# A hybrid decoder layer on one core: the value convolution's shifts from SBUF to SBUF in two rounds, and the inverse's natural rows read during the substitution

## The chip, the cores and the metric

The kernel runs on one core of a Trainium2 chip. The metric is the device time of one execution in microseconds. Each time shown is a median of runs on the chip; the profile is of one separate execution, with its own time beside it.

## The reference, cut to what matters

One layer, 256 tokens of width 2048, 256 memory tokens, float32. One projection of the normalised tokens gives q, k, v and two gates for a gated DeltaNet (24 value heads, 12 query and key heads of 128), the queries of a 4-head cross-attention into the memory, and a gate path z of width 4096. The branches are joined, multiplied by SiLU of z and sent through an output projection into the residual.

```
qkv = jax.nn.silu(causal_depthwise_conv(p[..., :c_qkv], conv_w))   # 4 taps along the tokens
m   = jnp.where(strict, beta * kk * decay, 0.0) + eye              # lower triangular, one per head and chunk
sol = lax.linalg.triangular_solve(m, rhs, left_side=True, lower=True, unit_diagonal=True)
y   = jnp.concatenate([mix, xa], axis=-1) * jax.nn.silu(z)
x   = x + jnp.einsum("bse,ed->bsd", y, w_out[i])
```

Two steps matter here. The depthwise convolution adds to each token's value three earlier tokens' values, each times a weight of its channel. And the triangular system of each head has to be inverted.

## The kernel before, in words

**Stream.** All weights flow through one pipeline, in the order of PLAN (line 55 on): blocks of 128 x 1024 numbers are loaded by SyncE's DMA queue into one of five `st` buffers (wraw, 278), cast on ScalarE into the upper part of one of four `wt` buffers (line 335), and VectorE subtracts to get the lower part (line 339). TensorE multiplies with both parts; twelve matmuls of 512 columns use up a block of the kinds V, K, x, v, z and o (proj_b), and a q or k tile takes two blocks (proj_a). LOOK keeps a few blocks ahead.

**Order.** The program is one stream of instructions, written by a small scheduler in Python. The big products set its clock `now`. Side work (convolutions, the inverse, the recurrence `delta`, the cross-attention) runs as generators that give up control with `yield`: a number is a delay in modelled microseconds, `pe_soon` (234) waits for what has been issued plus SLACK and then joins the queue for TensorE with a delay GATHER, `calm` (247) waits until VectorE's modelled backlog is under CALM. Each engine then executes its instructions in exactly the order in which they were written, and so does SyncE with its copies. Almost all operations are recorded through two helpers, so they have the lines 86 (TensorE, SyncE) and 103 (the others) in the profile; tiles are told apart by name.

**Values.** A v tile g (six of them) covers 512 value channels. Its matmuls end in two PSUM banks, one for each half r of 128 tokens, tokens on partitions (`v_done`, 1161). Since the tokens lie on partitions, a shift by tokens is a shift by partitions. For each half the value block `vs` is copied from PSUM, stored into a DRAM scratch `dv` with three rows of zeros ahead, and read back three times at offsets of one, two and three rows (`vsh`). Four weight rows, broadcast to all partitions, are loaded as `vw`. VectorE then does four products and three sums of 128 x 512, ScalarE the SiLU. `delta(g)` needs the two halves. `taps` (1147) prepares the weights in DRAM (`dtap`) and the rows of zeros in `dv`.

**Inverse.** `inverse(g)` runs twice, for 12 heads and two chunks each. `gram` writes the scaled matrices to DRAM (`dN`). The diagonal blocks of 32 x 32 are inverted by substitution on VectorE (`inN`, `inXT`, 31 steps), go through DRAM (`dY`, `dX`) into `Y` and `XN`, and then the natural rows of the whole matrices are read back as six tiles `n` of 128 x 512 (`n2`). After LAND, `merge` (1007) builds the 128 x 128 inverses on TensorE: 96 small matmuls `pm<-Y,n`, 72 pairs `pm<-Am,XN` and `pm<-XN,Am`, 48 + 48 larger ones. The second merge waits until `delta(2)` has used the first's `Y`.

Of the kernel before, what the change touches and what calls it, by code (L numbers as in the profile page):

```python
# [8 lines left out]
F32 = mybir.dt.float32  # L9
F32R = mybir.dt.float32r  # L10
AF = mybir.ActivationFunctionType
ALU = mybir.AluOpType
# [10 lines left out]
C = 128  # L23
# [9 lines left out]

LOOK = 2
WARM = 8
GATHER = 2.0
GATHER_Y = 4.0
XPACE = 3.0
HOP = 0.25
PINNED = 45.0  # L40
SLACK = 0.7
POLL = 0.3
CALM = 1.6
LAND = 6.0
VLAND = 5.0
INV_CALM = (1.2, 1.2)
GATE_CALM = 1.6
# [8 lines left out]
for _s in ("K0 K1 ab0 x0 x1 k0 k1 k2 k3 k4 k5 z6 z7 z0 z1 k6 k7 k8 v0 q0 q1 k9 k10 k11 v1 q2 q3 z2 v2 q4 q5 z3 v3 q6 q7 v4 q8 q9 v5 q10 q11 z4 z5 o0 o1 o2 o3").split():  # L56
    _kind = _s.rstrip("0123456789:")
    _t, _, _n = _s[len(_kind) :].partition(":")
# [14 lines left out]
def hybrid_kernel(ctx: ExitStack, tc: tile.TileContext, x, xT, memT, W, prm_d, cst_d, out):  # L73
# [51 lines left out]
    ve, se = Engine(nc.vector, ve_cost), Engine(nc.scalar, se_cost)  # L125
    po = Engine(nc.gpsimd, lambda e, op, a, k: 0.6)
# [8 lines left out]
    sd = Transfers()  # L135
# [7 lines left out]
    dp = ctx.enter_context(tc.tile_pool(name="dp", bufs=1, space=DRAM))  # L143

    def S2(name, shape, dt=F32):
        return s2p.tile([128] + list(shape), dt, name=name, tag="s2")
# [26 lines left out]
    def give(pt, t):  # L173

        idle[held.pop(id(pt))[0]].append(t)

    def bank(tag, name):
        yield from until(lambda: spare(tag))
        return PS(tag, name)
# [22 lines left out]
    def tr(o_, i_):  # L202
        now[0] += 0.093
        te.transpose(o_, i_, ident)
# [25 lines left out]
    def until(cond):  # L230
        while not cond():
            yield POLL

    def pe_soon(gather=0.0):

        yield max(fin[0] - now[0], 0.0) + SLACK
        yield "pe", gather
# [9 lines left out]
    def calm(queued=CALM):  # L247

        while ve.end > now[0] + queued:
            yield ve.end - now[0] - queued  # L250
# [677 lines left out]
    dN = [dp.tile([24, 129 * C], F32, name=f"dN{g}", tag=f"dN{g}") for g in range(2)]  # L928
# [3 lines left out]
    def mat(t):  # L932
        return t[:, 0 : C * C].rearrange("s (r c) -> s r c", c=C)

    def diag(t):

        return (t.rearrange("s (k e) -> (s k) e", k=4)[:, 0 : 32 * C]
                .rearrange("p (r c) -> p r c", c=C)[:, :, 0:32])

    def inverse(g):  # L940
        yield from until(lambda: all(p in grams for p in range(6 * g, 6 * g + 6)) and (g == 0 or "sub" in ready))
        yield 0.5
        nn = [S2("inN", [16, 32])[0:96] for _ in range(2)]
        xt = [S2("inXT", [16, 32])[0:96] for _ in range(2)]
        for f in range(2):
            sd.dma_start(nn[f], diag(dN[g])[:, 16 * f : 16 * f + 16])
        for f in range(2):
            po.memset(xt[f], 0.0)
        yield
        for f in range(2):  # L950
            po.memset(xt[f].rearrange("s c r -> s (c r)")[:, 16 * f : 512 : 33], 1.0)
        yield
        for i in range(1, 32):
            yield from calm(INV_CALM[g])
            work = []
            for f in range(2):
                w, j0 = min(16, i - 16 * f), 16 * f
                if w > 0:
                    tm = S2("inT", [16 * 32])[0:96]
                    work.append((f, w, j0, tm[:, 0 : w * (i - j0)].rearrange("s (c j) -> s c j", c=w)))  # L960
            for f, w, j0, tv in work:
                ve.tensor_tensor(out=tv, in0=xt[f][:, 0:w, j0:i],
                                 in1=nn[i // 16][:, i % 16, j0:i].unsqueeze(1).to_broadcast([96, w, i - j0]), op=ALU.mult)
            for f, w, j0, tv in work:
                ve.tensor_reduce(out=xt[f][:, 0:w, i], in_=tv, axis=AX.X, op=ALU.add)
            if len(work) == 1:
                ve.run(0.25)
        yield
        ready.add("sub")
        xn = nn  # L970
        for f in range(2):
            for e in range(2):
                ve.tensor_copy(xn[e][:, :, 16 * f : 16 * f + 16], xt[f][:, :, 16 * e : 16 * e + 16].rearrange("s c r -> s r c"))
        yield
        for f in range(2):
            sd.dma_start(dY[g][:, 16 * f : 16 * f + 16], xt[f])
        for f in range(2):
            sd.dma_start(dX[g][:, 16 * f : 16 * f + 16], xn[f])
        yield
        yield from until(lambda: g == 0 or "y5" in ready)  # L980
        nat = dX[g].rearrange("(s k) r c -> k r s c", k=4)
        tsp = dY[g].rearrange("(s k) r c -> k r s c", k=4)
        for k in range(4):
            b = slice(32 * k, 32 * k + 32)
            sd.dma_start(yall[b, :, b], tsp[k])
        for e in range(2):
            for k, r0, c0 in ((0, 64 * e, 0), (1, 64 * e + 32, 32), (2, 96 - 64 * e, 0)):
                sd.dma_start(xall[r0 : r0 + 32, e, :, c0 : c0 + 32], nat[k][:, 12 * e : 12 * e + 12])
        n2 = [S2("n2", [4, C]) for _ in range(6)]
        for i in range(6):  # L990
            sd.dma_start(n2[i], mat(dN[g])[4 * i : 4 * i + 4].rearrange("s r c -> r s c"))
        yield LAND
        yield from merge(g, n2)

# [147 lines left out]
    vss = [None] * 6  # L1142

    dtap = dp.tile([96, 128], F32, name="dtap", tag="dtap")
    dv = [dp.tile([259, 512], F32, name=f"dv{i}", tag=f"dv{i}") for i in range(2)]

    def taps():
        pt = yield from bank("m", "ptap")
        tr(pt[0:96, 0:128], prm[:, P_CW + 96 : P_CW + 192])
        yield 0.2  # L1150
        tp = S2("tp", [512])
        ve.memset(tp[:, 128:512], 0.0)
        se.copy(tp[0:96, 0:128], pt[0:96, 0:128])
        give(pt, se.end)
        yield
        sd.dma_start(dtap, tp[0:96, 0:128])
        for i in range(2):
            sd.dma_start(dv[i][0:3, 0:384], tp[0:3, 128:512])
            sd.dma_start(dv[i][0:3, 384:512], tp[0:3, 128:256])

    def v_done(g):

        raw, w = [None] * 2, []

        def done(r, pt):
            def go():
                yield 0.2
                v = raw[r] = S2("vs", [512])
                se.copy(v, pt)
                give(pt, se.end)  # L1170
                yield
                sd.dma_start(dv[g % 2][3 + 128 * r : 131 + 128 * r], v)
                if r == 0:
                    for j in range(4):
                        w.append(S2("vw", [4, 128]))
                        sd.dma_start(w[j], dtap.rearrange("(t k) c -> k t c", k=4)[3 - j][4 * g : 4 * g + 4]
                                     .unsqueeze(0).to_broadcast([128, 4, 128]))
                yield VLAND
                sh = [S2("vsh", [512]) for _ in range(3)]
                for j in (1, 2, 3):  # L1180
                    sd.dma_start(sh[j - 1], dv[g % 2][3 + 128 * r - j : 131 + 128 * r - j])
                wf = [t.rearrange("c t e -> c (t e)") for t in w]
                ve.tensor_tensor(out=v, in0=v, in1=wf[0], op=ALU.mult)
                yield VLAND
                for j in (1, 2, 3):
                    yield from calm()
                    ve.tensor_tensor(out=sh[j - 1], in0=sh[j - 1], in1=wf[j], op=ALU.mult)
                    ve.tensor_tensor(out=v, in0=v, in1=sh[j - 1], op=ALU.add)
                yield
                se.activation(v, v, AF.Silu)  # L1190
                vv = v.rearrange("c (w e) -> c w e", w=4)
                yield from until(lambda: all(p in grams for p in (2 * g, 2 * g + 1)))
                for h in range(4):
                    se.activation(vv[:, h, :], vv[:, h, :], AF.Copy, scale=sV[:, r, 4 * g + h : 4 * g + h + 1])
                yield
                raw[r] = vv
                ready.add(f"v{g}{r}")
                if r == 1:
                    vss[g] = raw
                    yield from delta(g)  # L1200
            spawn(go())
        return done

# [5 lines left out]
    def delta(g):  # L1209
# [6 lines left out]
        heads = [(w, w // 2, w % 2) for w in range(4)]  # L1216
        yield from pe_soon(GATHER)

# [16 lines left out]
        for i, p in enumerate(pp):  # L1235
            ve.tensor_tensor(out=kcl[:, i], in0=pkv[i][:, 0:4:2, :], in1=kch[:, i], op=ALU.subtract)
            give(pks[i], ve.end)
        yield from pe_soon(GATHER)
        A = yield from bank("A", "pU")
# [15 lines left out]
        ve.tensor_tensor(out=ul, in0=u0f, in1=uh, op=ALU.subtract)  # L1255
        yield from pe_soon(GATHER)
        yield from until(lambda: spare("A") and spare("B"))
# [17 lines left out]
        give(B, se.end)  # L1275
        yield from pe_soon(GATHER)
        yield from until(lambda: spare("A", 2))
# [13 lines left out]
        for i, p in enumerate(pp):  # L1291
            se.activation(q2[:, i, :], KQ[p][:, 1, :], AF.Square)
        yield from pe_soon(GATHER)
        yield from until(lambda: spare("B") and spare("m"))
# [179 lines left out]
```

## Time and profile before

| | |
|---|---|
| median of 3 runs | 873.8 us (873.25 to 876.49) |
| the profiled execution, its own time | 871.74 us |
| its span | 869.9 us |
| mean granted TensorE clock | 0.992 |
| busy: TensorE, VectorE, ScalarE, GpSimd | 854.2, 618.8, 535.7, 31.1 us |
| DMA | 187.9 MB, 216 GB/s over the span |
| copies of values: `dv<-vs`, `vsh<-dv`, `vw<-dtap` | 12, 36 and 24, of 256 KB each |
| natural rows `n<-dN` | 12 of 256 KB, issued from 317.6 to 543.1 us |

The first merge lies at 327 to 352 us of the span, the second at 549 to 566. The v tiles are worked on VectorE from about 349 to 654 us, between q tiles, z tiles and the recurrence; after 725 us there is only the output projection. A row of a group has the line, engine, operation, tiles written and read, shapes and count, then busy time and the mean of one in ns, then the idle time just before them and what ended it. A row of the windows has the length, the busy time of the engines with the number of instructions, the granted clock (1.00 is full), the busy share of the 16 DMA engines and GB/s. "issue" is time in which an engine waited for nothing that the profile shows.

### The profile page before, as it was taken

What the parts mean: (1) busy time and instruction counts of PE and PEld (TensorE: products, weight loads), DVE (VectorE), ACT (ScalarE), POOL (GpSimd) and SP (SyncE); (2) the same over time, 40 slices, a digit from 0 to 9 for tenths busy, and PEclk for the clock granted to TensorE, in tenths of its full rate; (3) what the DMA queues carried; (4) which work ended last, traced back from release to release, by engine and by line L of the source; (5) the groups of instructions that cost most, each with busy time, mean ns of one, the idle gap of its engine ahead of it and who ended that gap; (6) DMA issues with size and microseconds to landing.
All of it is one profiled execution on the core that took longest, in us unless ns stands there. A gap on an engine that the chain in (4) does not pass through costs nothing.

```text
span 869.9 us, 13113 instructions
## 1 busy us (share of the span) xinstructions
PE 854.2 (98%) x4789; PEld 716.0 (82%) x4789; DVE 618.8 (71%) x1081; ACT 535.7 (62%) x925; POOL 31.1 (4%) x33
## 2 busy tenths in 40 slices
PE   9999999999999998999999999799999999999998
PEld 6888888888888887888888888687888888888886
DVE  7778896657779954897988997359695665454542
ACT  7655755797644754896765775578776554333331
POOL 1000000000000000001000000000000000000000
PEclk9999999999999998999999999899999999999999
DMA  9865556448676686869869569767954538666650
GB/s 354 300 206 184 168 182 173 151 152 253 198 209 225 206 238 235 292 197 331 238 207 299 176 218 271 243 221 240 296 185 151 181 132 272 218 199 210 202 204 24
DMA packets 148239, 187.91 MB, mean 216 GB/s; under 512 B 24652, under 2 KB 115664, under 8 KB 148176
## 3 DMA queue, kind: packets, MB, share of 16 engines
q1 hardware_dynamic: 147744, 186.81, 66.5%
q8 instruction: 37, 0.61, 0.3%
q10 hardware_dynamic: 432, 0.28, 0.1%
q14 instruction: 26, 0.21, 0.1%
HBM read 177.01 MB, written 10.05 MB: 215 GB/s over the span
## 4 chain that ended last, share of the span: by engine, by line
PE 89%; ACT 5%; DMA 2%; issue 2%; DVE 2%; SPq 0%; POOL 0%; ACTq 0%; DVEq 0%
PE pb L86 68%; PE pa L86 12%; PE pO L86 2%; PE pU L86 1%; ACT wt L335 1%; PE pm L86 1%; ACT L103 1%; PE pkq L86 1%; ACT dec L103 1%; DVE wt L339 1%; DMA dv<-vs 1%; DMA vw<-dtap 1%; PE pyT L86 1%; PE pqs L86 1%; PE pkk L86 1%
## 5 line engine op out<-in xcount | busy, mean ns | idle before, releaser
L339 DVE TENSOR_TENSOR wt<-st,wt 128x1024 fp32r<-128x1024 f32 (+1 forms) x274 | 332.1, 1217 | 161.1 <-ACT wt L335 150.4
L335 ACT CAST wt<-st 128x1024 fp32r<-128x1024 f32 (+1 forms) x274 | 285.9, 1048 | 223.7 <-PE pb L86 184.1
L86 PE MATMUL pb<-wt,hkt 128*128 128x512 f32 x1536 | 361.6, 393 | 0.0
L86 PEld LDWEIGHTS pb<-wt,hkt 128*128 128x128 f32 x1536 | 286.7, 189 | 59.2
L86 PE MATMUL pb<-wt,yhi 128*128 128x512 f32 x512 | 158.1, 390 | 0.0
L86 PE MATMUL pa<-hkt,wt 128*128 128x512 f32 (+1 forms) x768 | 143.5, 343 | 0.4 <-DVE wt L339 0.3
L86 PEld LDWEIGHTS pa<-hkt,wt 128*128 128x128 f32 x768 | 118.9, 190 | 18.7 <-DVE wt L339 1.1
L86 PEld LDWEIGHTS pb<-wt,yhi 128*128 128x128 f32 x512 | 95.7, 188 | 19.6
L86 PE MATMUL pb<-wt,ylo 128*128 128x512 f32 x256 | 99.6, 389 | 0.0
L86 PE MATMUL pb<-wt,mkt 128*128 128x512 f32 x384 | 92.0, 400 | 0.9 <-ACT wt L335 0.7
L86 PEld LDWEIGHTS pb<-wt,mkt 128*128 128x128 f32 x384 | 73.6, 193 | 18.2 <-ACT wt L335 1.5
L86 PEld LDWEIGHTS pb<-wt,ylo 128*128 128x128 f32 x256 | 48.0, 188 | 10.1
L103 ACT ACT_TABLE_LOAD x29 | 37.2, 1283 | 5.7 <-DVE acc L103 5.3
L103 DVE SCALAR_TENSOR_TENSOR acc<-raw,prm,acc 128x255 f32<-128x255 f32 (+2 forms) x72 | 34.4, 478 | 1.4 <-ACT acc L103 1.0
L103 DVE TENSOR_TENSOR inT<-inXT,inN 96x1 f32<-96x1 f32 (+22 forms) x92 | 29.1, 342 | 3.0 <-DMA inN<-dN 2.3
L103 DVE TENSOR_REDUCE inXT<-inT 96x1 f32<-96x1 f32 (+22 forms) x92 | 28.6, 337 | 0.8
L103 DVE TENSOR_TENSOR vsh<-vsh,vw 128x512 f32<-128x512 f32 x36 | 24.1, 686 | 3.1 <-DMA vsh<-dv 3.1
L103 DVE TENSOR_TENSOR vs<-vs,vsh 128x512 f32<-128x512 f32 x36 | 24.7, 685 | 0.1
L103 POOL TENSOR_TENSOR e<-e,mhalf 128x8 f32<-128x8 f32 x6 | 10.5, 1748 | 288.9 <-DVE e L103 202.3
L103 ACT ACTIVATE dec<-erow,ngc 128x128 f32<-128x128 f32 x48 | 16.0, 394 | 4.0 <-DMA erow<-dgc 2.3
L103 ACT ACTIVATE dec<-erow,gcc 128x128 f32<-128x128 f32 x48 | 15.9, 396 | 3.5 <-DMA erow<-dgc 3.5
L103 DVE TENSOR_TENSOR vs<-vs,vw 128x512 f32<-128x512 f32 x12 | 8.2, 690 | 13.8 <-DMA dv<-vs 6.2
(202 smaller groups left out, 678.8 us busy)
## 6 DMA issues: line engine op xcount, KB each, us to landing
st<-W_d SPq DMA_DIRECT2D x272, 512.0 KB, 4.4
vsh<-dv SPq DMA_DIRECT2D x36, 256.0 KB, 6.2
erow<-dgc SPq DMA_DIRECT2D x24, 256.0 KB, 5.8
vw<-dtap SPq DMA_DIRECT2D x24, 256.0 KB, 6.0
dN<-dec SPq DMA_DIRECT2D x12, 256.0 KB, 2.9
n<-dN SPq DMA_DIRECT2D x12, 256.0 KB, 5.3
dv<-vs SPq DMA_DIRECT2D x12, 256.0 KB, 4.8
xraw<-xT_d SPq DMA_DIRECT2D x8, 256.0 KB, 5.7
```

The source lines that it names most:

```text
L86: return lambda *a, **k: pin(getattr(self.eng, op)(*a, **k))
L103: return pin(getattr(self.eng, op)(*a, **k))
L335: pin(se.eng.copy(hi[:, w] if parts > 1 else hi, st[:, w] if parts > 1 else src))
L339: pin(ve.eng.tensor_tensor(out=lo[:, w] if parts > 1 else lo, in0=st[:, w] if parts > 1 else src, in1=hi[:, w] if parts > 1 else hi, op=AL ...
```

## The change

Three things are changed, and three numbers.

The values' shifts no longer go through DRAM. With x1 the block shifted by one token, the four-tap sum is (w3 v + w2 x1), plus (w1 v + w0 x1) shifted by two tokens. So the first round copies `vs` one partition down inside SBUF (rows 0 to 126 to rows 1 to 127; the first row comes from the last row of the other half, or is a fill with zeros), and the second round copies the sum `t` two partitions down (126 rows, and two). The scratch `dv` and its rows of zeros are gone. The `vw` loads are issued before the values' copy.

The six natural row tiles `n` are requested one by one, from step 20 of the substitution, every second step, instead of all after the copies of `Y` and `XN`.

LAND, the time that a merge is held after its copies, goes from 6.0 to 9.0, SLACK from 0.7 to 1.0, GATHER, used in `delta`, from 2.0 to 0.5.

```
-GATHER = 2.0
+GATHER = 0.5
...
-SLACK = 0.7
+SLACK = 1.0
...
-LAND = 6.0
+LAND = 9.0
...
+            if i >= 20 and i % 2 == 0:
+                n2.append(S2("n2", [4, C]))
+                k = 4 * len(n2)
+                sd.dma_start(n2[-1], mat(dN[g])[k - 4 : k].rearrange("s r c -> r s c"))
...
-        n2 = [S2("n2", [4, C]) for _ in range(6)]
-        for i in range(6):
-            sd.dma_start(n2[i], mat(dN[g])[4 * i : 4 * i + 4].rearrange("s r c -> r s c"))
         yield LAND
...
-    dv = [dp.tile([259, 512], F32, name=f"dv{i}", tag=f"dv{i}") for i in range(2)]
...
+        def shift(dst, src, r, n):
+
+            sd.dma_start(dst[n:128], src[r][0 : 128 - n])
+            if r:
+                sd.dma_start(dst[0:n], src[0][128 - n : 128])
+            else:
+                po.memset(dst[0:n], 0.0)
...
                 yield
-                sd.dma_start(dv[g % 2][3 + 128 * r : 131 + 128 * r], v)
...
+                a, y, t = [S2("vc", [512]) for _ in range(3)]
+                shift(a, val, r, 1)
                 yield VLAND
-                sh = [S2("vsh", [512]) for _ in range(3)]
-                for j in (1, 2, 3):
-                    sd.dma_start(sh[j - 1], dv[g % 2][3 + 128 * r - j : 131 + 128 * r - j])
...
+                yield from calm()
...
+                ve.tensor_tensor(out=t, in0=v, in1=w1, op=ALU.mult)
+                ve.tensor_tensor(out=y, in0=a, in1=w0, op=ALU.mult)
+                ve.tensor_tensor(out=t, in0=t, in1=y, op=ALU.add)
+                two[r] = t
+                yield
+                yield from until(lambda: two[0] is not None)
+                b = S2("vc", [512])
+                shift(b, two, r, 2)
+                yield from calm()
+                ve.tensor_tensor(out=y, in0=v, in1=w3, op=ALU.mult)
+                ve.tensor_tensor(out=a, in0=a, in1=w2, op=ALU.mult)
+                ve.tensor_tensor(out=y, in0=y, in1=a, op=ALU.add)
                 yield VLAND
-                for j in (1, 2, 3):
-                    yield from calm()
-                    ve.tensor_tensor(out=sh[j - 1], in0=sh[j - 1], in1=wf[j], op=ALU.mult)
-                    ve.tensor_tensor(out=v, in0=v, in1=sh[j - 1], op=ALU.add)
+                yield from calm()
+                v = y
+                ve.tensor_tensor(out=v, in0=y, in1=b, op=ALU.add)
```

SyncE's queue at the first v tile, before: the stores and loads of the scratch, between weight loads (`st`), decay rows (`erow`) and the weights of the taps (`vw`).

```order
L86 DMA erow<-dgc 128x512
L86 DMA dv_113<-vs 128x512
L86 DMA vw<-dtap 128x4x128 x4
L86 DMA erow<-dgc 128x512
L86 DMA dv_113<-vs 128x512
L86 DMA st<-W_d 128x1024
L86 DMA vsh<-dv_113 128x512 x3
L86 DMA st<-W_d 128x1024
L86 DMA vsh<-dv_113 128x512 x3
```

The same place now; `vc` are the tiles of the new rounds.

```order
L86 DMA vw<-dtap 128x4x128 x4
L86 DMA st<-W_d 128x1024
L86 DMA erow<-dgc 128x512
L86 DMA vc<-vs 127x512 x2
L86 DMA vc<-vs 1x16x32
L86 DMA erow<-dgc 128x512
L86 DMA st<-W_d 128x1024 x3
L86 DMA st<-W_d 128x4x256
L86 DMA vc<-vc 126x512
L86 DMA erow<-dgc 128x512
L86 DMA st<-W_d 128x4x256
L86 DMA vc<-vc 126x512
```

The two copies of 127 rows, one for each half, stand next to each other, and each 126-row copy has weight loads before and behind it.

VectorE at the same place, before: `raw` and `acc` are the convolution of the q tile that follows.

```order
L339 TENSOR_TENSOR wt<-st,wt 128x1024 x6
L103 TENSOR_TENSOR vs<-vs,vw 128x512 x2
L103 TENSOR_TENSOR raw<-raw 128x256
L103 TENSOR_TENSOR vsh<-vsh,vw 128x512
L103 TENSOR_TENSOR vs<-vs,vsh 128x512
L103 TENSOR_TENSOR vsh<-vsh,vw 128x512
L103 SCALAR_TENSOR_TENSOR acc<-raw,prm,acc 128x255
L103 TENSOR_TENSOR vs<-vs,vsh 128x512
L103 SCALAR_TENSOR_TENSOR acc<-raw,prm,acc 128x254
L339 TENSOR_TENSOR wt<-st,wt 128x1024
```

VectorE now:

```order
L339 TENSOR_TENSOR wt<-st,wt 128x1024 x6
L103 TENSOR_TENSOR vc<-vs,vw 128x512
L103 TENSOR_TENSOR vc<-vc,vw 128x512
L103 TENSOR_TENSOR raw<-raw 128x256
L103 TENSOR_TENSOR vc<-vc 128x512
L103 TENSOR_TENSOR vc<-vs,vw 128x512
L103 TENSOR_TENSOR vc<-vc,vw 128x512
L103 SCALAR_TENSOR_TENSOR acc<-raw,prm,acc 128x255
L103 TENSOR_TENSOR vc<-vc 128x512
L103 SCALAR_TENSOR_TENSOR acc<-raw,prm,acc 128x254
L339 TENSOR_TENSOR wt<-st,wt 128x1024
```

The first `vc<-vc,vw` reads the first half's 127-row copy, the second the other half's; no subtraction of a weight block stands between the two.

SyncE's queue ahead of the second merge, before: the six `n` come after `Y` and `XN`, in one run.

```order
L86 DMA vsh<-dv_114 128x512 x3
L86 DMA Y<-dY_107 32x24x32 x4
L86 DMA XN<-dX_109 32x12x32 x6
L86 DMA n_5384<-dN_105 128x4x128
L86 DMA n_5385<-dN_105 128x4x128
L86 DMA n_5386<-dN_105 128x4x128
```

Now they lie between weight loads, ahead of the copies into `dY`:

```order
L86 DMA n_4967<-dN_105 128x4x128
L86 DMA st<-W_d 128x4x256 x2
L86 DMA n_5004<-dN_105 128x4x128
L86 DMA erow<-dgc 128x512
L86 DMA st<-W_d 128x1024
L86 DMA erow<-dgc 128x512
L86 DMA n_5078<-dN_105 128x4x128
L86 DMA st<-W_d 128x1024 x3
```

The last of the six stands between the two 127-row copies of the fourth v tile.

More of the change, by code (lines that the diff above doesn't have):

```diff
@@ L952, in inverse @@
         yield
+        n2 = []
         for i in range(1, 32):
@@ L1150, in taps @@
         yield 0.2
-        tp = S2("tp", [512])
-        ve.memset(tp[:, 128:512], 0.0)
-        se.copy(tp[0:96, 0:128], pt[0:96, 0:128])
+        tp = S2("tp", [128])
+        se.copy(tp[0:96], pt[0:96, 0:128])
         give(pt, se.end)
         yield
[L1156 to L1159, printed above, removed]
+        sd.dma_start(dtap, tp[0:96])
     def v_done(g):
-        raw, w = [None] * 2, []
+        raw, w, val, two = [None] * 2, [], [None] * 2, [None] * 2
+        def shift(dst, src, r, n):
[4 more added lines that the diff above has]
+                po.memset(dst[0:n], 0.0)
         def done(r, pt):
@@ L1167, in go @@
                 yield 0.2
-                v = raw[r] = S2("vs", [512])
+                v = val[r] = S2("vs", [512])
                 se.copy(v, pt)
                 give(pt, se.end)
-                yield
-                sd.dma_start(dv[g % 2][3 + 128 * r : 131 + 128 * r], v)
                 if r == 0:
@@ L1177, in go @@
                                      .unsqueeze(0).to_broadcast([128, 4, 128]))
+                yield
+                a, y, t = [S2("vc", [512]) for _ in range(3)]
+                shift(a, val, r, 1)
                 yield VLAND
-                sh = [S2("vsh", [512]) for _ in range(3)]
-                for j in (1, 2, 3):
-                    sd.dma_start(sh[j - 1], dv[g % 2][3 + 128 * r - j : 131 + 128 * r - j])
-                wf = [t.rearrange("c t e -> c (t e)") for t in w]
-                ve.tensor_tensor(out=v, in0=v, in1=wf[0], op=ALU.mult)
+                yield from calm()
+                w3, w2, w1, w0 = [t_.rearrange("c t e -> c (t e)") for t_ in w]
+                ve.tensor_tensor(out=t, in0=v, in1=w1, op=ALU.mult)
+                ve.tensor_tensor(out=y, in0=a, in1=w0, op=ALU.mult)
+                ve.tensor_tensor(out=t, in0=t, in1=y, op=ALU.add)
+                two[r] = t
+                yield
+                yield from until(lambda: two[0] is not None)
[5 more added lines that the diff above has]
+                ve.tensor_tensor(out=y, in0=y, in1=a, op=ALU.add)
                 yield VLAND
-                for j in (1, 2, 3):
-                    yield from calm()
-                    ve.tensor_tensor(out=sh[j - 1], in0=sh[j - 1], in1=wf[j], op=ALU.mult)
-                    ve.tensor_tensor(out=v, in0=v, in1=sh[j - 1], op=ALU.add)
+                yield from calm()
+                v = y
+                ve.tensor_tensor(out=v, in0=y, in1=b, op=ALU.add)
                 yield
```

## The prediction

> **What bounds the kernel now.** I read the page's busy shares first, then the chain that ended last, the waits, the windows of 20 us, and the DMA part.
>
> ```profile
> span 869.9 us, 13113 instructions
> PE 854.2 (98%) x4789; PEld 716.0 (82%) x4789; DVE 618.8 (71%) x1081; ACT 535.7 (62%) x925; POOL 31.1 (4%) x33
> PE 89%; ACT 5%; DMA 2%; issue 2%; DVE 2%; SPq 0%; POOL 0%; ACTq 0%; DVEq 0%
> 725.39 140.79 PE pb L86 x621
> 551.83 4.61 issue
> ```
>
> TensorE is busy 98% of the span, and the chain runs through it for 89%. The last piece of the chain gives its undisturbed pace: 140.79 us over 621 matmuls is 0.227 us each, so a weight block of 12 matmuls lasts 2.72 us. Whatever leaves TensorE fed costs nothing; whatever starves it adds to the time one for one.
>
> ```profile
> 320.00:340.00 20.00, 16.91 (x299) 14.27 (x298) 7.51 (x19) 8.93 (x18) 1.01 (x1) 0.83 0.73 248
> 520.00:540.00 20.00, 20.00 (x119) 17.55 (x118) 14.86 (x26) 11.39 (x25) 0.00 (x0) 1.00 0.93 286
> 540.00:560.00 20.00, 14.82 (x287) 12.27 (x286) 11.91 (x24) 11.36 (x29) 1.64 (x1) 0.88 0.92 296
> 560.00:580.00 20.00, 19.87 (x172) 15.97 (x171) 7.93 (x8) 16.13 (x31) 0.00 (x0) 0.95 0.36 112
> ```
>
> After the span's first slices the two real holes are the merges, at 330 to 338 and 549 to 557 us (columns: PE, PEld, DVE, ACT, POOL, granted clock, DMA share, GB/s). In each, TensorE stood still for some microseconds and then ran at a lower granted clock: 0.83 of 20 us is 3.4 us lost, and 0.88 with 0.95 is 2.4 + 1.0 = 3.4 us. So a hole of 4 to 5 us costs itself and 3.4 us of slow clock.
>
> ```profile
> ACT wt L335 <- PE pb L86: 184.1, 134, 3.5
> DVE wt L339 <- ACT wt L335: 150.4, 119, 5.4
> SPq L86 <- DVE wt L339: 391.1, 171, 10.9
> L339 DVE TENSOR_TENSOR wt<-st,wt 128x1024 fp32r<-128x1024 f32 (+1 forms) x274 | 332.1, 1217 | 161.1 <-ACT wt L335 150.4
> L335 ACT CAST wt<-st 128x1024 fp32r<-128x1024 f32 (+1 forms) x274 | 285.9, 1048 | 223.7 <-PE pb L86 184.1
> ```
>
> This is the cover that feeds it. The cast of a block waits 134 times for TensorE to free one of the four wt buffers: three blocks lie between a freed buffer and its next use, 3 x 2.72 = 8.2 us, of which cast and subtraction take 1.05 + 1.22. A finished block is thus at most 5.9 us early, and 3.2 us just before the next is made: 4.5 us on average. If VectorE stops, TensorE runs dry some 4.5 us later.
>
> **What the change does to the copies.** The DRAM round goes: 12 stores of values and 36 shifted loads. In their place stand 12 copies of 127 rows, 12 of 126 and twelve of one or two rows. How long does a 127-row copy take?
>
> ```profile
> DMA packets 148239, 187.91 MB, mean 216 GB/s; under 512 B 24652, under 2 KB 115664, under 8 KB 148176
> q1 hardware_dynamic: 147744, 186.81, 66.5%
> q10 hardware_dynamic: 432, 0.28, 0.1%
> ...
> st<-W_d SPq DMA_DIRECT2D x272, 512.0 KB, 4.4
> ...
> dv<-tp SPq DMA_DIRECT2D x2, 4.5 KB
> dv<-tp SPq DMA_DIRECT2D x2, 1.5 KB
> dgc<-gc SPq DMA_DIRECT2D x1, 24.0 KB
> ...
> dgl<-gc SPq DMA_DIRECT2D x1, 0.1 KB
> glb<-dgl SPq DMA_DIRECT2D x1, 12.0 KB
> ```
>
> The packet counts tell how rows are shared out. Queue 10 carried three copies of 128 rows: 432 = 3 x 128 + 3 x 16, so each ends in 16 small packets, one per engine. Now all packets under 512 B: 24,652, less 16,896 rows of 128 B (8 Y copies x 768, 12 XN x 384, 4 inN x 1,536), 128 rows of glb, 128 of prm and 24 elements of dgl, leaves 7,476 closing packets. The list of issues has 471 copies. The 465 of 32, 96 or 128 rows give 7,440; the 36 left are four copies of 3 rows with 3 each and the two of 24 rows with 12 each. So 24 rows run on 12 engines, two each, not on 16. Every copy in the program has equal shares on at most 16 engines. 127 is a prime: its only equal share is all on one engine. Rounded-up shares (8 rows on 15 engines, 7 on the last) would explain the 24 rows as well; no copy here tells these apart. I take equal shares, since nothing else was ever seen.
>
> The Trainium skill ("DMA: Bandwidth & Descriptors", section "Why a DMA increments its semaphore by 16 and not by 1") says that a copy issued from SyncE takes the largest number up to 16 that divides the rows, and that 127 rows go to one engine. The closing packets agree with it for 3 and 24 rows; by rounding up instead, the sum would be that of the first rival.
>
> ```profile
> 554.00:556.00 2.00, 0.00 (x0) 0.81 1.02 403
> DMA to landing us min/median/max: 3.0/5.6/7.5
> ```
>
> The first row is a 2 us window of TensorE (clock, DMA share, GB/s): 403 GB/s at 1.02 of 16 engines is 24.7 GB/s an engine; queue 1 over the run gives 186.81 MB / (0.665 x 16 x 869.9 us) = 20.2. 127 rows of 2 KB are 260,096 B: 10.5 us on one engine, or 12.9. The second row is that of the tile dv: its copies land 3.0 us after issue at best, of which 0.7 is moving, so 2.3 us come on top. The first copy lands 12.8 us after issue. The second (the other half of the tokens) stands right behind it on SyncE and on the same engine: 23.3 us. I take the faster rate, since these are long packets.
>
> ```profile
> 347.28 1.37 SPq L86 DMA_DIRECT2D vsh<-dv  x3
> 354.37 0.68 DVE L103 TENSOR_TENSOR vsh<-vsh,vw 128x512 f32<-128x512 f32 x1
> L103 DVE TENSOR_TENSOR vsh<-vsh,vw 128x512 f32<-128x512 f32 x36 | 24.1, 686 | 3.1 <-DMA vsh<-dv 3.1
> ```
>
> VectorE uses a shifted copy some 7.1 us after its issue (VLAND is still 5.0 and the calm limit 1.6); for copies landing in 6.2 us that was right, and it waited 3.1 us in all. Now it stands from +7 until +12.8 for the first copy, and then, with no subtraction of a weight block between the two products in five groups of six, until +23.3 for the second. Behind it lie the q tile's additions and the subtractions that feed TensorE. On SyncE the 126-row copy waits for VectorE's sum, with weight loads behind it; loads that were issued have a sixteenth of their rows behind the two copies on that engine.
>
> TensorE runs dry at 7 + 4.5 = 11.5 and gets its next block at 23.3 + two more operations of 0.69 + 1.22, about 26: 14.5 us idle. With the longest cover (5.9) and a block squeezed in between (2.72), and the subtraction next in line, it is 24.5 - 15.6 = 8.9. I take the middle, 11.7, and 3.4 us of slow clock: 15.1 us a group, 90.6 us for six. Ends: 6 x 8.9 = 53; with 12.9 us a copy, the second landing at 28.1, 6 x (30.7 - 11.5 + 3.4) = 136.
>
> **The other parts.** VectorE's work on the values stays: seven operations of 0.69 us a half, before and after. The 12 fills on GpSimd are some 0.3 us each on an engine busy 4%: nothing. The bytes fall by 24 x 256 KB, 3% of 187.9 MB, hidden while TensorE is full.
>
> ```profile
> DVE vs L103 <- DMA dv<-vs: 6.2, 3, 2.6
> DVE vs L103 <- DMA vw<-dtap: 5.5, 4, 2.5
> PE pU L86 <- DVE ul L103: 0.9, 1, 0.9
> PE pm L86 <- issue: 6.0, 2, 4.6
> q8 instruction: 37, 0.61, 0.3%
> ```
>
> The waits of VectorE that go (6.2 and, as vw is now asked for before the shift, 5.5) stand where TensorE was full: 520 to 540 has 20.00 of 20. I count nothing, 1 us of gain at most. GATHER and SLACK place delta's matmuls about 1 us sooner; TensorE's longest wait there was 0.9 us, so -1 to +3, taken as 0.
>
> The natural inverse rows (six copies of 256 KB a merge) now go out between weight loads, and LAND holds the merge 3 us more; SyncE waited 391 us for VectorE anyway, so their issue is covered. What do they save? TensorE's 4.61 us in the second merge stood in the middle of one run of 72 small matmuls, behind no semaphore. PE has 2 x 4789 instructions; 37 packets on the instruction queue are one per 259 of them, so this is most likely a late block of instructions, while DMA stood at 1.02. In the first merge, with DMA quieter, that wait was shorter:
>
> ```profile
> 334.25 0.53 PE L86 MATMUL pm<-Am,XN 32*32 32x32 f32 x19 [1.42 <-issue]
> 556.44 0.25 PE L86 MATMUL pm<-Am,XN 32*32 32x32 f32 x1 [4.61 <-issue]
> ```
>
> With 1.5 MB less in flight I take the second down to the first: -3.2. Ends: 0, and -8 if hole and slow clock both go. The Trainium skill ("Runtime: NRT & Kernel Launch", section "Instruction fetch mechanics") calls crossing such a block mostly hidden; the 4.61 us speak against that here, and by the page this term would be 0.
>
> **Sum.** On the profiled execution, 871.7 us with 869.9 of span: 871.7 + 90.6 - 3.2 = 959. It lies 2 us below the median of the runs shown, 873.8; I do not add them. About 0.5%, 4.4 us, is what a measurement can tell from no change.
>
> **The rivals.** *Rounded-up shares, faster.* The 127 rows go as 8 to an engine and land like dv's copies, at 5.6 us; VectorE's wait stays nil. Then the merges (-3.2, perhaps -8) and up to 1 us of removed waits remain: 871.7 - 3.2 - 1 = 867.5, between 862 and 871. For it: 24 rows on 12 engines fits. Against it: no unequal share in 471 copies. It decides if the copies land under 7 us. Chance 0.20.
>
> *No change.* Landing is quick, but the second merge's hole is a fetch of instructions that comes late whatever the other copies do: 872, between 868 and 876. For it: the first merge has such a hole with little DMA. Chance 0.08.
>
> *Late copies, mostly absorbed.* One engine moves SBUF rows faster than any row here shows, 7 us a copy: the second lands at 16.3, TensorE is idle for 16.3 + 2.6 - 11.5 = 7.4 less one block of 2.7, too short for the slow clock: 6 x 4.7 - 3.2 = +25, 897. Against it: both rates from the trace are below that. Chance 0.07.
>
> That the builder cuts the 127 rows into parts by itself is not so: the list of SyncE's instructions has them whole, while the single row is cut into 16 parts.
>
> **The numbers.** The forecast, 959, has 0.65; its own range is 915 (53 - 8 on top) to 1005 (136 less 3). Forecast and absorbed case make slower 0.72, the first rival faster 0.20, the second no change 0.08. To leave out no more than 2 in 10, the range reaches down through the rivals, 864, and stops at 990, above which I see some 0.07, with 0.05 below.
>
> **What would show it.** Right: the 127-row copies landing at 12 us and more, VectorE waiting for vc of a shift copy in each of six groups, holes of 9 to 15 us in PE with a clock under 1 after each, and weight loads landing late beside them. In the merge: an issue wait under 2 us in the second. Wrong: landings of 127 rows near 6 us, with PE full between 340 and 620 us but for the merges.

## The result, and the profile after

| | before | after |
|---|---|---|
| median of 4 runs each | 875.13 us (873.25 to 876.49) | 944.88 us (940.93 to 948.84) |
| ratio, with its 95% interval | | 1.0799 [1.0746, 1.0851] |
| the profiled execution, and its span | 871.74, 869.9 us | 948.84, 947.1 us |
| mean granted TensorE clock | 0.992 | 0.955 |

The change makes the kernel 8% slower. First the page of the changed kernel: the span, the busy shares, the forty slices of TensorE and of its clock, the DMA sum, the shares of the chain.

```profile
span 947.1 us, 13137 instructions
PE 868.1 (92%) x4789; PEld 724.3 (76%) x4789; DVE 620.4 (66%) x1080; ACT 538.2 (57%) x927; POOL 44.0 (5%) x45
PE   8999999999999997967997996965949999999998
PEclk8999999999999997986998997997979999999999
DMA packets 144737, 181.58 MB, mean 192 GB/s; under 512 B 24256, under 2 KB 115256, under 8 KB 144672
PE 76%; DMA 12%; ACT 4%; DVE 3%; issue 2%; SPq 1%; ACTq 0%; DVEq 0%
```

TensorE has the same 4,789 matmuls and no longer fills its slices between 350 and 710 us; the dents are the places of the v tiles, and the clock dips with them. DMA is 12% of the chain (2% before), with less to move. The chain, in order of time (start, length), names a decay row in the first of the six groups and the copies of 127 rows in the other five:

```profile
349.71 10.18 DMA erow<-dgc
404.85 13.95 DMA vc<-vs
491.18 18.67 DMA vc<-vs
566.27 18.70 DMA vc<-vs
627.60 17.88 DMA vc<-vs
682.54 17.72 DMA vc<-vs
```

TensorE's timeline has a hole at each group, in the fourth a second one of 2.55 us ahead of the one shown (start and length of the piece, in brackets the idle time before it and what ended it):

```profile
361.32 13.82 PE L86 MATMUL pa<-hkt,wt 128*128 128x512 f32 x64 [7.71 <-ACT raw L103]
432.39 2.07 PE L86 MATMUL pO<-u,aT 128*128 128x128 f32 x8 [15.46 <-ACT u L103]
513.21 6.99 PE L86 MATMUL pb<-wt,hkt 128*128 128x512 f32 x22 [6.88 <-DVE wt L339]
588.34 6.54 PE L86 MATMUL pb<-wt,hkt 128*128 128x512 f32 x20 [6.09 <-DVE wt L339]
649.09 5.46 PE L86 MATMUL pb<-wt,hkt 128*128 128x512 f32 x14 [17.02 <-DVE wt L339]
703.26 1.94 PE L86 MATMUL pyT<-cst,xa 128*128 128x128 f32 x8 [13.04 <-DVE kcl L103]
```

VectorE's timeline shows the wait that was forecast. In the last four groups it stands once for each of the two copies (the second group and three of these four are shown):

```profile
429.10 0.69 DVE L103 TENSOR_TENSOR vc<-vc,vw 128x512 f32<-128x512 f32 x1 [16.50 <-issue]
499.56 0.69 DVE L103 TENSOR_TENSOR vc<-vc,vw 128x512 f32<-128x512 f32 x1 [4.92 <-DMA vc<-vs]
509.94 0.69 DVE L103 TENSOR_TENSOR vc<-vc,vw 128x512 f32<-128x512 f32 x1 [4.55 <-DMA vc<-vs]
574.10 0.69 DVE L103 TENSOR_TENSOR vc<-vc,vw 128x512 f32<-128x512 f32 x1 [6.93 <-DMA vc<-vs]
585.07 0.69 DVE L103 TENSOR_TENSOR vc<-vc,vw 128x512 f32<-128x512 f32 x1 [6.88 <-DMA vc<-vs]
633.42 0.69 DVE L103 TENSOR_TENSOR vc<-vc,vw 128x512 f32<-128x512 f32 x1 [8.05 <-DMA vc<-vs]
645.94 0.69 DVE L103 TENSOR_TENSOR vc<-vc,vw 128x512 f32<-128x512 f32 x1 [10.29 <-DMA vc<-vs]
```

In the first group it waits only 1.93 us. In the second it stands 16.50 us; the profile names no releaser there, but the chain has the first copy landing at 418.8 us and the product starting 10.3 us later, which fits the second copy.

In the three groups shown with both waits the second product follows the first by 10.4, 11.0 and 12.5 us. In the first of them nothing is issued between the two copies, so 10.4 us is the time of one copy on its engine, 82 ns a row of 2 KB; in the others a natural row tile and a weight load stand between. The waits of the changed kernel (us in total, times, longest) have more in them than that, though:

```profile
DVE vc L103 <- DMA vc<-vs: 60.5, 9, 10.3
ACT acc L103 <- DVE raw L103: 46.1, 6, 16.8
PE pb L86 <- DVE wt L339: 33.4, 6, 17.0
ACT wt L335 <- DMA st<-W_d: 20.7, 7, 9.2
ACT dec L103 <- DMA erow<-dgc: 16.0, 6, 11.8
```

ScalarE waits for weight blocks and decay rows too; before, these two lines had 2.0 and 5.8 us. And SyncE's own timeline shows something that no row of before has:

```profile
404.85 6.19 SPq L86 DMA_DIRECT2D vc<-vs  x3
411.08 9.31 SPq L86 DMA_DIRECT2D erow<-dgc  x1
485.27 15.99 SPq L86 DMA_DIRECT2D vc<-vs  x3
568.19 8.05 SPq L86 DMA_DIRECT2D st<-W_d  x1
```

Behind the second copy, one single issue lasts 6.8 to 10.1 us in every group: a decay row in the second, a weight load in the fourth, and in the other four the single row that belongs to the copies. Before, the longest issue of `st` took 1.67 and of `erow` 1.79 us. So three waits grew at the same places: VectorE's for the copies, ScalarE's for loads behind them, SyncE's inside an issue. The trace alone does not say which of them holds TensorE.

**Are the 127 rows on one engine?** The packets under 512 B say so. Of 24,256, 16,896 are the rows of 128 B counted in the prediction, 96 the six single rows (cut in 16 each), 128, 128 and 24 the others counted there. Left are 6,984 closing packets. The other copies give 417 x 16 + 2 x 12 (24 rows) + 6 x 16 (single rows, cut) + 6 x 2 (two rows) = 6,804. The last 180 are 12 x 1 + 12 x 14: 127 rows on one engine, 126 on 14. Shares rounded up would need 12 x 16 + 12 x 16 = 384. This is what the Trainium skill states ("DMA: Bandwidth & Descriptors", section "Why a DMA increments its semaphore by 16 and not by 1"), and here the trace agrees with it to the packet.

### The profile page after: what moved, and what is told of

The parts are those of the page before. It is cut to its first block, busy times and chain, and to the rows that moved or that the text cites. A ratio compares the mean times of both kernels' runs of the same rounds, so it can differ in the third digit from the quotient of the medians.

```text
span 947.1 us, 13137 instructions
## 1 busy us (share of the span) xinstructions
PE 868.1 (92%) x4789; PEld 724.3 (76%) x4789; DVE 620.4 (66%) x1080; ACT 538.2 (57%) x927; POOL 44.0 (5%) x45
## 2 busy tenths in 40 slices
DMA packets 144737, 181.58 MB, mean 192 GB/s; under 512 B 24256, under 2 KB 115256, under 8 KB 144672
## 4 chain that ended last, share of the span: by engine, by line
PE 76%; DMA 12%; ACT 4%; DVE 3%; issue 2%; SPq 1%; ACTq 0%; DVEq 0%
PE pb L86 63%; DMA vc<-vs 9%; PE pa L86 6%; DMA erow<-dgc 2%; SPq L86 1%; DVE wt L339 1%; PE pU L86 1%; PE pO L86 1%; ACT wt L335 1%; DVE vc L103 1%; PE pm L86 1%; ACT dec L103 1%; PE pyT L86 1%; PE pkq L86 1%; DMA mst<-memT_d 1%
## 5 line engine op out<-in xcount | busy, mean ns | idle before, releaser
L86 PE MATMUL pb<-wt,hkt 128*128 128x512 f32 x1536 | 372.0, 400 | 32.6 <-DVE wt L339 32.6
L86 PEld LDWEIGHTS pb<-wt,hkt 128*128 128x128 f32 x1536 | 292.5, 193 | 95.9 <-DVE wt L339 34.8
L103 DVE TENSOR_TENSOR vc<-vc,vw 128x512 f32<-128x512 f32 x24 | 16.5, 687 | 77.0 <-DMA vc<-vs 60.5
L86 PEld LDWEIGHTS pb<-wt,ylo 128*128 128x128 f32 x256 | 48.1, 188 | 10.1
L103 ACT ACTIVATE acc<-raw,prm 128x256 f32<-128x256 f32 x24 | 12.1, 505 | 46.1 <-DVE raw L103 46.1
L86 PE MATMUL pO<-u,aT 128*128 128x128 f32 x96 | 13.7, 288 | 15.5 <-ACT u L103 15.5
L86 PEld LDWEIGHTS pO<-u,aT 128*128 128x128 f32 x96 | 12.8, 203 | 16.2 <-ACT u L103 15.9
L103 DVE TENSOR_TENSOR vc<-vc 128x512 f32<-128x512 f32 x36 | 24.6, 684 | 0.1
```

The source lines that it names most:

```text
L86: return lambda *a, **k: pin(getattr(self.eng, op)(*a, **k))
L103: return pin(getattr(self.eng, op)(*a, **k))
```

## The experiments

All kernels compute the whole layer. The times are medians; ratios are to the kernel before on the same chip.

**The copies in shares.** The changed kernel, with each long copy cut in a part of 112 rows and the rest:

```
-            sd.dma_start(dst[n:128], src[r][0 : 128 - n])
+            sd.dma_start(dst[n : n + 112], src[r][0:112])
+            sd.dma_start(dst[n + 112 : 128], src[r][112 : 128 - n])
```

> The changed kernel with each shifted copy cut so that its rows divide: 127 as 112 + 15, 126 as 112 + 14. Theory (equal shares: 127 rows run on one engine): copies land near 6 us, VectorE's waits for them fall from 60.5 + 16.5 us to under 8, the six holes of TensorE go, 862 to 870 us. Rival A (rows moved from SBUF to SBUF are slow, or the two rounds are a chain that is too long): holes stay, over 920 us. Rival B (the merges or the three numbers cost the time): over 920 us too, with the copies landing early.

Measured: 861.93 us, ratio 0.9859 [0.9835, 0.9882]. Its page:

```profile
span 860.5 us, 13169 instructions
PE 850.8 (99%) x4789; PEld 711.3 (83%) x4789; DVE 619.4 (72%) x1080; ACT 538.1 (63%) x927; POOL 46.5 (5%) x45
PE   8999999999999999999999999999999999999998
```

Two lines of its waits:

```profile
DVE vc L103 <- DMA vc<-vs: 2.9, 2, 2.1
ACT wt L335 <- DMA st<-W_d: 0.6, 2, 0.3
```

No dent is left, at the v tiles or at the merges. One more copy of 15 rows per long copy turns the loss into a gain: the whole loss lies in how the rows are shared out, 83 us between this kernel and the changed one. It beats both other kernels, and is the version to keep.

**Values alone, merges alone.** One kernel has the values' part of the change and nothing else; the other has the natural rows, LAND, SLACK and GATHER as changed, with the values through DRAM as before. The first takes from the diff of the change all that concerns `dv`, `shift` and the two rounds. Its core:

```
-                sd.dma_start(dv[g % 2][3 + 128 * r : 131 + 128 * r], v)
...
+                shift(a, val, r, 1)
...
+                shift(b, two, r, 2)
```

> The kernel before with the values' change alone (natural rows, LAND, SLACK and GATHER as before). Theory: all of the loss is in the 127-row copies, so the time is that of the changed kernel plus what the merges gained, 945 to 958 us. Rival B (merges or numbers cost the time): 870 to 885 us.

Measured: 963.48 us, 1.1017 [1.0992, 1.1042], 5.5 us above the theory's range. VectorE's wait for the copies is 60.6 us, as in the changed kernel. The second kernel:

```
-GATHER = 2.0
+GATHER = 0.5
...
-SLACK = 0.7
+SLACK = 1.0
...
-LAND = 6.0
+LAND = 9.0
...
+            if i >= 20 and i % 2 == 0:
+                n2.append(S2("n2", [4, C]))
...
-        n2 = [S2("n2", [4, C]) for _ in range(6)]
```

> The kernel before with the rest of the change alone (natural rows early, LAND 9, SLACK 1.0, GATHER 0.5; values through DRAM). Theory: a gain at the merges only, 3 to 10 us, 864 to 872 us; no slow clock after 330 us. Rival B: 920 us and more. Rival C (the merge's hole is independent of other copies): 874 us.

Measured: 866.17 us, 0.9906 [0.9887, 0.9924]. So the values' part is the loss, and the rest by itself a gain of 9.0 us. One part of the expectation did not come: the clock is still 0.80 from 560 to 580 us. Between values alone and the whole change lie 18.6 us, twice that; why the other edits are worth more beside late copies was not tried.

**Is it the path from SBUF to SBUF, or the number of rows?** The kernel before, with the DRAM scratch; only the load at offset one is cut in 127 rows and one:

```
-                    sd.dma_start(sh[j - 1], dv[g % 2][3 + 128 * r - j : 131 + 128 * r - j])
+                    m = 127 if j == 1 else 128
+                    sd.dma_start(sh[j - 1][0:m], dv[g % 2][3 + 128 * r - j : 3 + m + 128 * r - j])
+                    if m < 128:
+                        sd.dma_start(sh[j - 1][m:128], dv[g % 2][3 + m + 128 * r - j : 131 + 128 * r - j])
```

> The kernel before with one change: of the three loads from the DRAM scratch, the one shifted by one row is cut into 127 rows and one row. Theory (the number of rows decides, not where they lie): two loads of 10.7 us on one engine in each group, as in the changed kernel, 925 to 960 us. Rival A (SBUF to SBUF is what is slow): 872 to 880 us.

Measured: 960.43 us, 1.0981 [1.0952, 1.1009], 0.4 us above the range. From its waits:

```profile
DVE vsh L103 <- DMA vsh<-dv: 75.1, 11, 10.6
ACT wt L335 <- DMA st<-W_d: 48.9, 12, 9.1
```

And the packets of its page:

```profile
DMA packets 148071, 187.91 MB, mean 196 GB/s; under 512 B 24484, under 2 KB 115496, under 8 KB 148008
```

A kernel that never copies from SBUF to SBUF loses as much. The number of rows is the cause: 24,652 - 24,484 = 168 closing packets fewer are 12 x 16 gone and 12 x 1 + 12 x 1 new ones, one engine for 127 rows and one for the single row.

**How much for each row?** The split kernel, with the first round cut in 61 + 66 and in 97 + 30 rows. 61 and 97 are primes; the rest is as in the split kernel.

```
-            sd.dma_start(dst[n : n + 112], src[r][0:112])
-            sd.dma_start(dst[n + 112 : 128], src[r][112 : 128 - n])
+            c = 61 if n == 1 else 112
+            sd.dma_start(dst[n : n + c], src[r][0:c])
+            sd.dma_start(dst[n + c : 128], src[r][c : 128 - n])
```

> The cut kernel (112 + 15, 112 + 14) with the first round cut as 61 + 66 rows instead: 61 is a prime and goes to one engine, 5.1 us at 24.7 GB/s. Theory (time of the rows on one engine): the second half's copy lands at 2 x 5.1 + 2.3 = 12.4 us, 5 us late for VectorE, which the finished weight blocks mostly cover: 862 to 876 us. Rival D (a row number that does not divide costs a fixed amount, by its semaphores or set-up): as with 127 rows, about 945 us.

Measured: 889.45 us, 1.0163 [1.0123, 1.0203]: a miss, 13 us above the range. The prediction's own formula does better than that range: the copy landing at 12.4, 2.6 us of VectorE behind it and TensorE dry at 11.5 leave 3.5 us a group, 21 us in all; TensorE's idle time in the profile is 27.7 us against 9.7 in the split kernel, 18.0 more.

> As f_dose61 with 97 + 30 rows: 97 on one engine, 8.0 us a copy. Theory: the second copy lands at 18.4 us instead of 23.4, 5 us a group less than with 127 rows, where a group lost (945 - 862) / 6 = 13.8 us: 6 x 8.8 = 53 us over the cut kernel, 900 to 925 us. Rival D: 945 us.

Measured: 922.53 us, 1.0541 [1.0486, 1.0596], within it. Above the split kernel's 861.93, 61, 97 and 127 rows on one engine cost 27.5, 60.6 and 83.0 us: 0.92 us a row over the first step, 0.75 over the second, and 55.5 / 66 = 0.84 from 61 to 127, where twelve copies have 12 x 82 ns = 0.98 us of work a row on the engine. The doses are not quite pure. The closing packets, 228 and 180 fewer than in the split kernel (24,580 and 24,628 packets under 512 B, 24,808 there), are those of 66 rows on 11 engines and 30 rows on 15, so the engine with the long part may have carried 6 or 2 rows more; the records do not tell engines apart. Followed down, the line from 61 to 127 meets zero at 61 - 27.5 / 0.84 = 28 rows, 4.6 us of two copies a group; with those rows counted it is 37 rows and 6.1 us. This is an extrapolation from two runs for each dose, not a measured cover. It lies near the cover of 4.5 us in the prediction.

**VectorE's order, or the loads behind the copies?** Theory 1 is the prediction's: VectorE stands at the product, and the subtractions that feed TensorE stand behind it. Theory 2: weight blocks and decay rows behind the two copies come late, whatever VectorE does. The changed kernel, with VectorE's products written 20 modelled us after the copies:

```
                 shift(a, val, r, 1)
-                yield VLAND
+                yield 20.0
```

> The changed kernel, 127 rows whole, with the products after the first round held 20 us instead of 5, so that VectorE need not wait for the copies. Theory 1 (VectorE standing in order is nearly all of the loss): 862 to 885 us, VectorE's waits for vc under 15 us. Theory 2 (weight loads with a sixteenth of their rows behind the copies on the one engine, and SyncE's queue behind them, are the loss as well): 895 to 945 us with ScalarE's casts waiting for st.

Measured: 964.36 us, 1.1018 [1.099, 1.1045], above the range of either theory. Its waits:

```profile
ACT wt L335 <- DMA st<-W_d: 94.4, 11, 20.3
PE pb L86 <- ACT wt L335: 40.1, 6, 12.7
ACT dec L103 <- DMA erow<-dgc: 17.4, 5, 11.9
```

And one issue from SyncE's timeline:

```profile
411.98 10.04 SPq L86 DMA_DIRECT2D st<-W_d  x1
```

VectorE no longer waits for a first-round copy at all: that line is gone from the list. The time is 19.5 us worse, not 60 or more better. Theory 1 alone falls, and ScalarE's waits for `st` are those that theory 2 names; why the time lies 19 us above theory 2's range is open. Later products might have cost something of their own, so the other side was tried: copies that nobody waits for. The split kernel, with one added:

```
                 shift(a, val, r, 1)
+                sd.dma_start(dummy[r][1:128], v[0:127])
```

`dummy` is a DRAM scratch that is never read.

> The split kernel, with a copy of 127 rows that nobody reads added behind each first-round copy (the values into a DRAM scratch). VectorE never waits for these copies, and 127 rows land about 10.5 us after their turn on their one engine. Theory 1 (the order of VectorE alone: a product waits for its copy, the subtractions stand behind): nobody waits for the new copies, so 862 to 870, with PE full from 340 to 720 us. Theory 2 (what lies behind the 127-row copies on their engine, weight blocks and decay rows, is what starves TensorE): two such copies a group as in the changed kernel's first round, so about 930 to 965, with ScalarE waiting for weight blocks and decay rows for 80 us and more, and VectorE's wait for a shifted copy only where that copy itself stands behind the dummy.

Measured: 940.14 us, 1.076 [1.0736, 1.0784], in theory 2's range; ScalarE's two waits are 63.1 + 14.3 = 77.4 us, a little under the 80 expected. Its waits:

```profile
ACT wt L335 <- DMA st<-W_d: 63.1, 9, 15.8
DVE vc L103 <- DMA vc<-vs: 32.8, 6, 8.4
PE pb L86 <- DVE wt L339: 21.7, 8, 12.1
ACT dec L103 <- DMA erow<-dgc: 14.3, 5, 9.0
```

SyncE's timeline at the second group:

```profile
407.15 0.24 SPq L86 DMA_DIRECT2D dummy<-vs  x1
407.49 6.32 SPq L86 DMA_DIRECT2D vc<-vs  x5
413.85 0.42 SPq L86 DMA_DIRECT2D dummy<-vs  x1
414.33 8.42 SPq L86 DMA_DIRECT2D erow<-dgc  x1
```

Copies without a reader cost 78 us over the split kernel. VectorE's wait has not gone with the reader: of its 32.8 us, 31.7 are for shared copies that stand behind a dummy on SyncE's queue. The issue right behind the second dummy lasts 8.42 us, and the weight load after it comes only then. So two long copies on one engine starve TensorE through whatever stands behind them, weight loads, decay rows and VectorE's own shared copies. That VectorE's wait isn't needed for a loss is shown by the held products above, where it is absent and TensorE waits 40.1 us for ScalarE's casts. How much VectorE's wait would cost with the loads on time was not tried, nor how the loss divides between late issues and late rows.

**What in the merges gains 9 us?** Four kernels took some of these edits into the kernel before; the kernel with all of them, 866.17 us, is the comparison. Natural rows alone:

```
+            if i >= 20 and i % 2 == 0:
+                n2.append(S2("n2", [4, C]))
...
-        n2 = [S2("n2", [4, C]) for _ in range(6)]
```

> The kernel before with the natural rows early and nothing else. Theory (less traffic at the merge shortens the late instruction block): 868 to 873 us, the issue wait of the second merge under 2 us. Rival (the merge only has to be later): 874 us.

Measured: 875.68 us, 1.001 [0.9984, 1.0035]: no gain, as the rival has it. LAND 9.0 alone:

```
-LAND = 6.0
+LAND = 9.0
```

> The kernel before with LAND at 9.0 alone. If the later merge is what the three edits beside the values gain (the trio measured 866.2 against 875.1, the natural rows alone 875.7): about 868, with the 4.6 us hole of the second merge gone. If SLACK and GATHER carry it, or only all together: 873 to 877.

Measured: 876.21 us, 1.0013 [0.9994, 1.0031]. SLACK 1.0 and GATHER 0.5 alone:

```
-GATHER = 2.0
+GATHER = 0.5
...
-SLACK = 0.7
+SLACK = 1.0
```

> The kernel before with SLACK 1.0 and GATHER 0.5 alone. If TensorE joins side work later and so waits less for its results: about 868 to 871, with fewer small waits in the merges and in delta. If LAND carries the gain: 873 to 877.

Measured: 878.15 us, 1.004 [1.0014, 1.0066], above both ranges. Natural rows and LAND, the first two of these together:

```
+            if i >= 20 and i % 2 == 0:
+                n2.append(S2("n2", [4, C]))
...
-LAND = 6.0
+LAND = 9.0
```

> The kernel before with the early natural rows and LAND at 9.0, without SLACK and GATHER. If the early rows and the hold work only together (rows land before the merge's first product): about 866 to 868. If the hold alone does it, the same as that kernel; if SLACK and GATHER do, 873 to 877.

Measured: 868.22 us, 0.9926 [0.99, 0.9951]. So neither edit gains alone, and the pair gains 0.74%, 6.2 us by the medians. SLACK and GATHER cost 3.7 us alone, and on top of the pair are worth 2 us or nothing: 0.9906 and 0.9926 have overlapping intervals. Single profiles give a hint why the natural rows alone don't pay. TensorE's timeline in the second merge with natural rows alone:

```profile
551.04 0.31 PE L86 MATMUL pm<-Am,XN 32*32 32x32 f32 x2 [1.93 <-ACT Am L103]
560.14 0.33 PE L86 MATMUL pm<-Y,n 64*64 64x64 f32 x2 [1.66 <-ACT Y L103]
```

The wait on issue, 4.61 us before, is gone; in its place in this execution TensorE waits for ScalarE's copies of `Am` and `Y`. With LAND 9.0 alone the issue waits stay (2.7 us in the two merges). With both, the window of the first merge (columns as in the prediction) has no hole at all, where before it had 16.91 of 20 at a clock of 0.83:

```profile
325.00:345.00 20.00, 20.00 (x270) 16.21 (x270) 8.43 (x10) 10.19 (x17) 0.00 (x0) 1.00 0.76 238
```

But the natural rows alone already have 20.00 of 20 at 1.00 in that window, and the second merge of the kernel with both still waits 3.04 us once for `Y`. So what LAND adds is not located by these profiles; that the pair gains stands on the medians.

## Why the prediction was right, and where it wasn't

**Shares: right.** Equal shares, so all of 127 on one engine, was taken against the rounded-up rival because no other share had been seen in 471 copies. The closing packets, the split kernel and the cut DRAM load settle it. The 10.5 us a copy was worked out from the rate per engine of a 2 us window in the merge; 10.4 us came where nothing stood between the two copies, up to 12.5 where a load did. That also ends the rival with 7 us a copy.

**TensorE's loss per group: right in size.** The split kernel is the same program with the rows shared, so the difference is the price of the long copies. The idle time is 947.1 - 868.1 = 79.0 us in the one and 860.5 - 850.8 = 9.7 in the other: 69.3 us, or 11.5 a group, where 11.7 was forecast. The same matmuls are busy 868.1 - 850.8 = 17.3 us longer, which goes with the lower clock, 0.955 against 0.996 in the profiles: 2.9 a group, where 3.4 was forecast. Together 86.6 us in the profiles and 83.0 in the medians, for 90.6. That the mean comes so close is partly luck. The forecast took every group at the middle of 8.9 and 14.5 us; the main holes are 7.7, 15.5, 6.9, 6.1 (with one of 2.6 ahead of it), 17.0 and 13.0, so only the last lies between. The prediction also saw no subtraction of a weight block between the two products in five groups; there is one in two groups, the third and the fourth, and these have the shortest of the main holes.

**The path to TensorE: half right.** The step that failed is the one that led from the late copies to TensorE by VectorE alone: it "stands from +7 until +12.8 for the first copy, and then [...] until +23.3 for the second", and behind it "the subtractions that feed TensorE". VectorE does stand so, and in five groups the chain of the changed kernel runs through its product. But the kernel whose VectorE never waits for these copies, and the one whose long copies nobody reads, lose 102 and 78 us against the split kernel. Neither is a clean price of the loads: the first also works the values later, and in the second VectorE still waits 32.8 us. The prediction named the loads "behind the two copies on that engine" and gave them no price. It missed the issue entirely: it called each load's share late, while in fact SyncE stands 7 to 10 us at a single issue in each group. The size came out all the same, most likely because both paths last as long as the two copies, so that taking away one leaves the other; that is argued, not measured. By the step as written, a later product should have gained 60 us and more; it lost 19.5.

**The merges: mis-sized, and the reason incomplete.** The term was -3.2, for natural rows that take traffic from the second merge. All edits beside the values gave -9.0. The mechanism is there: in every kernel that asks early, TensorE's wait on issue at `pm` is 1.3 us or less, and without it 2.7 to 6.0. But alone it bought nothing, and the prediction counted LAND as covered when it was the other half of the gain. That the wait is a late block of instructions stays an argument; no run shows it.

**Two slips.** The low end of the forecast's own range, 871.7 + 53 - 8 us, is 917 and not 915. And the rival of absorbed copies took holes of 4.7 us as "too short for the slow clock", where the prediction's own rows charge 3.4 us of it to holes of 4 to 5 us; in the kernel with all merge edits the clock is 0.80 from 560 to 580 us behind a hole of only 1.65.

**GATHER and SLACK, 0: about right.** +3.7 alone, -2 or nothing with the others.

**The removed DRAM round, 0 to 1: too small.** The split kernel stands 4.2 us below the one with all merge edits and the DRAM round; the intervals, 0.9882 at most and 0.9887 at least, just miss each other. The latter's profile has one hole of 1.65 us at 556.7 us with the lower clock behind it, and the split kernel's has none over 1 us there. Whether the round's copies made that hole was not tried.

The sum: 90.6 - 83.0 = 7.6 us too much for the copies and 9.0 + 4.2 - 3.2 = 10.0 too little for the rest, less 3.4 because the median before is 875.13 and not the 871.7 from which the forecast starts. That is the 14 us between 959 and 944.88.

## What to carry to other kernels

Look at the number of rows of every copy before its bytes: 127 rows cost some 83 us here where 112 + 15 gain 13 against the kernel before. When one engine is overloaded, ask what lies behind it on the issuing queue, and not only who waits for that copy: letting the reader come later did not help, and copies without a reader cost about as much. And try edits to a schedule in pairs before dropping one of them: two that gain nothing alone gained 0.74% together.

## What the runs showed of the hardware that was not expected

An engine's backlog reaches the issuing queue. With two copies of 127 rows ahead, single issues on SyncE lasted up to 9.31 us (`erow`), 8.05 (`st`) and 10.08 (`vc`), against 1.8 at most before for `st`, `erow`, `dv` and `vsh`. The list of SyncE's copies by tile (duration of the issue in ns: least, median, most) for the `st` loads of the changed kernel:

```profile
L86 SPq DMA_DIRECT2D st<-W_d x274: 327/367/8047, 0.7 to 921.1; - x137
```

and of the split kernel:

```profile
L86 SPq DMA_DIRECT2D st<-W_d x274: 327/367/1770, 0.7 to 834.7; - x137
```

The medians are equal; only the loads behind a long copy are held. SyncE issues in order, so a load behind a held issue is late with all its rows, also with those that the other fifteen engines would have moved. In all six groups the issue held behind the second copy ends 1.4 to 3.0 us after the first copy has landed (in the second group by the chain, in the others by the start of VectorE's first product). What holds the issue, the records don't name.
